# Down's first operands asked for as slots come free, a second buffer for block 21, no block of four pairs, x2 added one product later

## The chip, the cores and the metric

The kernel runs on one core of a Trainium2 chip. The metric is the device time of one execution in microseconds (us); the profile of one execution shows, for each engine, when every instruction ran and what it waited for. PE is the matrix engine, DVE, ACT and POOL are the vector, scalar and GpSimd engines, and SP issues nearly all DMAs, strictly in the order of its queue.

## What is computed

One layer of a decoder trunk on 512 tokens of width 2048, in float32. The part that matters here is the feed-forward network at its end:

```python
x = x + mix @ w_out[l]                      # x2 in the kernel
h2 = _rms_norm(x, norm2_g[l])
x = x + (jax.nn.silu(h2 @ w_gate[l]) * (h2 @ w_up[l])) @ w_down[l]
```

with 5632 hidden columns: `w_gate` and `w_up` are 2048 x 5632, `w_down` is 5632 x 2048. Ahead of it stand a norm, one input projection, three token mixers and the output projection.

## The kernel before

Everything is kept transposed, 128 channels on the partitions and 512 tokens along a row. Each float32 operand is split in a high and a low part; a product is high x (high and low) and low x high. In the feed-forward network the matrix products are done by a seven-product scheme of Strassen's kind: the token axis and the two channel axes are cut in halves, and seven products of halves (numbered q, taken in the order 5 1 7 6 2 4 3) take the place of eight. One product over a "pair" (two 128-channel tiles, one of each half) is one matmul `wh` of 128x512, against the operand's high and low parts side by side, and one `wl` of 128x256.

**Weights.** A block of products needs four weight blocks, named 11, 12, 21 and 22, read from memory into raw buffers of 128x1024, and three sums of them that POOL makes: s = 21 + 22, later s + 11, later s + 12, and 21 + 11 in place (line 184; "s+11" and "s+12" in the text). The seven products take, in order, s, 11, 21, s, 12, 22, s. Each is then split: ACT writes a copy `wn` to PSUM (L248) and `wh` to one of three buffers (L249), and DVE writes `wl` (L229). PE reads wh and wl (L988). A raw buffer is free again once its block has been split for the last time or added. Before the change 22 and s have two buffers (a and b, for even and odd blocks of products), and 21, 11 and 12 have one. `pump` asks SP for the entries in list order (L219), and stops at the first whose buffer is taken.

**Slots.** All other tiles (128x512 float32) come from a pool of 75 slots. A new tile takes a slot that has been given back; its first writer waits until the last user of the old tile is done. An operand load that waits so holds all that is behind it in SP's queue.

**The stages at the end.** Gate/up walks 22 pairs of hidden tiles p in `GU_ORDER`, which ends with 21, 0 and 5; each p is two blocks, g (gate) and u (up), of seven products over the 8 pairs of `ops`, the operand tiles, which stay in 56 slots throughout. The result of a p becomes seven operand tiles a (one per q), which are stored to memory (`od<-a`, L962) one after another as they are computed during the next blocks. Pairs 0 and 5 (`STAY`) are also kept in slots; pair 5 is not stored.

Down then runs 25 blocks d0 to d24, given by the table `DOWN`: (n, first, end) adds the pairs first to end-1 to the output rows n and n+8. Rows 0 to 7 are visited three times (row 0 four times); between visits the partial sums y go to memory and back (`yd<-y` L1121, `y<-yd` L1100). Block d16 is (0, 12, 18), six pairs; d21 is (0, 18, 22), four pairs. At the last visit of a row x2 is loaded (L1103), and POOL adds it to y at the block's start (L1116, L1117), ahead of that block's s+11.

**The order around the change.** The functions run product by product. Ahead of each product come the sums that are due (`sums_now`) and the evacuations of the product before (`evacs`); behind it come `extras`, a second list, with DMAs. `later(n, ...)` puts a call n products further on. In u5, the last gate/up block, each product gives back its eight `ops` slots, and one product later four operands of the same q are loaded for d0 (`load_act`, L1168: pairs 1 to 4 for each q, 28 loads in all). In Down the pairs that the next block adds are loaded likewise, product by product, and y and x2 of the next block are asked for after the fourth product.

Of the kernel before, what the change touches and what calls it, by code (L numbers as in the profile page):

```python
# [9 lines left out]
F32 = mybir.dt.float32  # L10
# [7 lines left out]
T = 512  # L18
# [28 lines left out]

N_SLOTS = 75

RAW_PLAIN = "22b sb 21 22a 11 sa 12".split()  # L50
RAW_BUFS = 7
RAW_EARLY = 5
# [22 lines left out]
        (0, 5, 12), (1, 6, 14), (2, 7, 15), (3, 8, 16), (4, 9, 17), (5, 10, 18), (6, 11, 19), (7, 13, 20),  # L75
        (0, 12, 18), (1, 14, 22), (2, 15, 22), (3, 16, 23), (4, 17, 24), (0, 18, 22), (5, 18, 25), (6, 19, 26), (7, 20, 27)]

# [40 lines left out]
def kernel(ctx: ExitStack, tc: tile.TileContext, xT, wi, wo, wgu, wd, cst_in, outT):  # L118
# [46 lines left out]
    for u, unit in enumerate(units):  # L165
        entries.append((RAW_PLAIN[u % RAW_BUFS], u, [unit]))
        works.append((u, True, nc.vector))

    def group(name, m, n, blocks):

        key = {k: (k, name) for k in ("11", "12", "21", "22", "s")}
        for k in ("21", "22", "11", "12"):
            entries.append((k + "ab"[m] if k == "22" else k, key[k], blocks[k]))
        u = len(works)
# [794 lines left out]
    class Block:  # L969
# [3 lines left out]
        def __init__(self, name, m):  # L973
            self.name = name

            self.banks = dict(zip((5, 1, 7, 6), outs if m == 0 else (outs[3], outs[1], outs[2], outs[0])))
            self.banks.update({3: self.banks[5], 4: self.banks[7], 2: self.banks[1]})

        def multiply(self, q, w, xs):
# [23 lines left out]
    class Wide(Block):  # L1003
# [55 lines left out]
        def piece(self, at, src):  # L1059
# [3 lines left out]
            for k in range(n):  # L1063
                q, s = LAID[at + k], slice(k * TH, (k + 1) * TH)
                t = slot(f"a{q}_{self.p}", F32R)
                nc.scalar.copy(t[:, :TH], src[:, s])
                nc.vector.tensor_sub(t[:, TH:], src[:, s], near[:, s].bitcast(F32))
                if self.p in STAY:
                    acts[q, self.p] = t
                if self.p != STAY[1]:  # L1070
                    later(0, nc.sync.dma_start, od[self.p][:, (at + k) * T:(at + k + 1) * T], t.bitcast(F32),
                          queue=extras)
# [18 lines left out]
    def visit(t):  # L1091

        return [all(w[0] != DOWN[t][0] for w in part) for part in (DOWN[:t], DOWN[t + 1:])]

    def load_y(t):
        if t < len(DOWN):
            for n in (DOWN[t][0], DOWN[t][0] + 8):
                y[t, n] = slot(f"y{t}_{n}")
                if not visit(t)[0]:
                    nc.sync.dma_start(y[t, n], yd[n])  # L1100
                if visit(t)[1]:
                    xr[n] = slot(f"yx{n}")
                    nc.sync.dma_start(xr[n], x2d[n])  # L1103

    class Down(Block):


        def __init__(self, t):
            super().__init__(f"d{t}", t % 2)
            self.n = DOWN[t][0]  # L1110
            self.fresh, last = visit(t)
            self.out = outT if last else yd
            self.tail = t == len(DOWN) - 1
            self.y1, self.y2 = y.pop((t, self.n)), y.pop((t, self.n + 8))
            if last:
                nc.gpsimd.tensor_add(self.y2, self.y2, xr.pop(self.n + 8))  # L1116
                nc.gpsimd.tensor_add(self.y1, self.y1, xr.pop(self.n))  # L1117

        def store(self, n, t, cols):
            def go():  # L1120
                nc.sync.dma_start(self.out[n][:, cols], t[:, cols])  # L1121
            if self.tail:
                go()
            else:
                later(0, go, queue=extras)

# [35 lines left out]
    def load_act(q, pairs):  # L1162
        for j in pairs:
            if (q, j) in acts or j == STAY[1]:
                continue
# [5 lines left out]
    for g in range(2 * NP + len(DOWN)):  # L1171
# [8 lines left out]
        for i, q in enumerate(ORDER):  # L1180
# [10 lines left out]
            if t == -1:  # L1191
                for j in range(NJ):
                    ops.pop((q, j))
                later(1, load_act, q, range(*DOWN[0][1:]), queue=extras)
            elif 0 <= t < len(DOWN) - 1:
                for j in range(FIRST[t], FIRST[t + 1]):
                    acts.pop((q, j))
                later(1, load_act, q, range(LAST[t], LAST[t + 1]), queue=extras)
            if t >= -1 and i == 3:
                load_y(t + 1)  # L1200
# [86 lines left out]
```

## Time and profile before

| | |
|---|---|
| median of 3 runs | 1910.57 us (1910.22 to 1911.08) |
| the profiled execution | 1910.5 us, of it span 1908.7 us |
| PE busy | 1892.0 us, 99% |
| DVE, ACT, POOL busy | 1466.9 us, 1330.1 us, 995.6 us |
| mean granted PE clock | 0.997 |
| DMA | 320.29 MB, mean 168 GB/s |

Gate/up runs up to about 1465 us and Down from there to the end. A row of the timeline gives start, duration, engine, line, operation, output and inputs, shape and count, and in brackets the idle time before it with what ended it. "SPq" is the issue of a DMA, whose duration is not that of the transfer. In the windows a row gives the stretch, PE's busy time, the granted clock (1.00 is full rate), the DMA engines' busy share and GB/s.

### The profile page before, as it was taken

The page shows a single profiled execution, that of the slowest core. Times are in us where ns is not written, and L with a number is a line of the kernel's source. Part 1 is how long each engine was busy: PE and PEld are TensorE (multiplying, and loading weights), DVE is VectorE, ACT ScalarE, POOL GpSimd, SP SyncE. Part 2 cuts the span into 40 slices and gives each one's busy share as a digit, 9 for nine tenths or more (in the row PEclk, how much of TensorE's full clock was granted, in tenths as well). Part 3 has the DMA queues.
Part 4 walks back from the last instruction along what each step waited for, and adds up shares of the span by engine and source line. Part 5 has one row for each costly group of instructions (what it writes and reads, how often), then busy time and mean ns, then how long its engine had stood idle before and what let it go on. Part 6 is the DMA issues. An engine that isn't in the chain of part 4 may idle for free. (4 is left out here: it accounts for less than half of the span.)

```text
span 1908.7 us, 29643 instructions
## 1 busy us (share of the span) xinstructions
PE 1892.0 (99%) x10342; PEld 1639.4 (86%) x10342; DVE 1466.9 (77%) x2561; ACT 1330.1 (70%) x1855; POOL 995.6 (52%) x643
## 2 busy tenths in 40 slices
PE   9999999999999999999999999999999999999999
PEld 7888888878888888888888888888888888888887
DVE  6789988998679777777777777777777777677766
ACT  6356655553357888888888887888887777766765
POOL 0111011000002887787878877788666655655766
PEclk9999999999999999999999999999999999999999
DMA  7342242333332344444435443444438777776876
GB/s 266 88 128 78 83 130 77 110 107 129 117 137 101 124 162 141 160 160 157 158 130 182 147 167 137 161 164 159 152 136 289 248 244 251 272 251 236 294 263 214
DMA packets 136309, 320.29 MB, mean 168 GB/s; under 512 B 15584, under 2 KB 31072, under 8 KB 136160
## 3 DMA queue, kind: packets, MB, share of 16 engines
q1 hardware_dynamic: 136016, 318.31, 49.2%
q8 instruction: 81, 1.33, 0.3%
q14 instruction: 68, 0.56, 0.1%
q10 hardware_dynamic: 144, 0.10, 0.0%
HBM read 254.11 MB, written 55.84 MB: 162 GB/s over the span
## 5 line engine op out<-in xcount | busy, mean ns | idle before, releaser
L988 PE MATMUL out<-h,wh 128*128 128x512 f32 x2464 | 588.8, 391 | 1.0 <-DVE h L899 0.8
L988 PEld LDWEIGHTS out<-h,wh 128*128 128x128 f32 x2464 | 452.7, 188 | 89.3 <-DVE h L899 1.3
L988 PEld LDWEIGHTS out<-h,wl 128*128 128x128 f32 x2464 | 316.0, 191 | 12.0
L988 PE MATMUL out<-h,wl 128*128 128x256 f32 x2464 | 319.9, 283 | 0.0
L988 PE MATMUL out<-a,wh 128*128 128x512 f32 x1232 | 298.4, 392 | 3.8 <-ACT wh L249 2.5
L988 PEld LDWEIGHTS out<-a,wh 128*128 128x128 f32 x1232 | 226.1, 189 | 49.2 <-ACT wh L249 3.3
L242 ACT CAST wh<-w 128x1024 fp32r<-128x1024 f32 (+1 forms) x93 | 96.8, 1041 | 113.9 <-PE o L272 49.0
L988 PEld LDWEIGHTS out<-a,wl 128*128 128x128 f32 x1232 | 161.8, 194 | 8.9 <-DVE wl L229 2.0
L988 PE MATMUL out<-a,wl 128*128 128x256 f32 x1232 | 164.6, 285 | 1.3 <-DVE wl L229 1.2
L229 DVE TENSOR_TENSOR wl<-w,wh 128x1024 fp32r<-128x1024 f32 (+1 forms) x93 | 112.4, 1209 | 44.6 <-ACT wh L242 44.4
L458 DVE SCALAR_TENSOR_TENSOR y<-bu,cst,y 128x511 f32<-128x511 f32 (+14 forms) x120 | 89.6, 747 | 0.2
L1000 DVE TENSOR_TENSOR y<-y,out 128x256 f32<-128x256 f32 x93 | 39.1, 420 | 39.3 <-PE out L988 37.1
L271 PE MATMUL cq<-hh,wh 128*128 128x512 f32 x128 | 51.2, 400 | 0.5 <-DVE mix_c L743 0.5
L271 PE MATMUL o<-mh_c,wh 128*128 128x512 f32 x128 | 51.6, 403 | 0.0
L273 PE MATMUL o<-mh_c,wl 128*128 128x512 f32 x128 | 50.5, 394 | 0.0
L272 PE MATMUL o<-ml_c,wh 128*128 128x512 f32 x128 | 50.4, 394 | 0.0
L273 PE MATMUL cq<-hh,wl 128*128 128x512 f32 x128 | 50.0, 391 | 0.0
L272 PE MATMUL cq<-hl,wh 128*128 128x512 f32 x128 | 50.0, 390 | 0.0
L1001 DVE TENSOR_TENSOR y<-y,out 128x256 f32<-128x256 f32 x101 | 42.5, 421 | 3.5
L386 POOL TENSOR_TENSOR lvr<-lvv,nhalf 128x4 f32<-128x4 f32 x1 | 1.9, 1928 | 76.6 <-DVE lvv L385 76.6
L184 POOL TENSOR_TENSOR w('s', 'g1')_5687<-w('21', 'g1')_5484,w('22', 'g1')_5533 128x1024 f32<-128x1024 f32 x1 | 2.5, 2453 | 71.0 <-DVE wl L229 71.0
L849 DVE TENSOR_TENSOR xr<-xr,o 128x512 f32<-128x512 f32 x32 | 21.8, 682 | 13.8 <-PE o L273 13.7
(3135 smaller groups left out, 4867.4 us busy)
## 6 DMA issues: line engine op xcount, KB each, us to landing
a<-od SPq DMA_DIRECT2D x175, 256.0 KB, 5.4
od<-a SPq DMA_DIRECT2D x147, 256.0 KB, 3.2
w<-in_wi SPq DMA_DIRECT2D x59, 512.0 KB, 3.6
w<-in_wo SPq DMA_DIRECT2D x32, 512.0 KB, 3.5
yd<-y SPq DMA_DIRECT2D x68, 128.0 KB, 3.0
y<-yd SPq DMA_DIRECT2D x34, 256.0 KB, 5.3
x<-in_xT SPq DMA_DIRECT2D x16, 256.0 KB, 7.2
xr<-in_xT SPq DMA_DIRECT2D x16, 256.0 KB, 3.8
```

The source lines that it names most:

```text
L184: eng.tensor_add(out[:, :n], raws[key[a]][0][:, :n], raws[key[b]][0][:, :n])
L229: fn(*args)
L242: nc.scalar.copy(hi[:, :n], t[:, :n])
L271: nc.tensor.matmul(out, wh, xh, start=start, stop=False)
L272: nc.tensor.matmul(out, wh, xl, start=False, stop=False)
L273: nc.tensor.matmul(out, wl, xh, start=False, stop=stop)
L386: nc.gpsimd.tensor_tensor(r, v, nhalf[:, :NT], op=ALU.pow)
L458: nc.vector.scalar_tensor_tensor(yconv[j][:, i:], hconv[j][:, :T - i], c, yconv[j][:, i:], op0=ALU.mult, op1=ALU.add)
L849: nc.vector.tensor_add(t, t, b)
L988: nc.tensor.matmul(out, lhs[:, s], rhs, start=begin, stop=x is xs[-1] and low == flip[0], skip_group_check=True)
L1000: sign(out, out if first is None else first, main)
L1001: sign(out, out, rest)
```

## The change

- The raw buffer of 21 becomes two (21a and 21b), paid for with two slots (73 instead of 75); block 22 stands ahead of 21 in the list.
- The operands of d0 are asked for earlier: those of product 5 during g5, the block before u5; the others during u5's first four products, in the numbers in which the products give back slots.
- Pair 0 is no longer stored in gate/up but product by product during d0, from the slots in which it stays.
- d16 becomes (0, 12, 17) and d21 (0, 17, 22): five pairs each.
- For rows 0 and 8 x2 is added in d8 instead of the last visit; in all blocks that add x2 the additions come one product later, and y and x2 of the next block are asked for after the second product instead of the fourth.
- The stores of y are put one product later.
- The four PSUM banks are handed on from block to block by a rule instead of by the block's parity; the rotation is the same.

```diff
-N_SLOTS = 75
+N_SLOTS = 73
-RAW_PLAIN = "22b sb 21 22a 11 sa 12".split()
-RAW_BUFS = 7
+RAW_PLAIN = "22b sb 21a 22a 11 sa 12".split()
+RAW_BUFS = 8
...
-        (0, 12, 18), (1, 14, 22), (2, 15, 22), (3, 16, 23), (4, 17, 24), (0, 18, 22), (5, 18, 25), (6, 19, 26), (7, 20, 27)]
+        (0, 12, 17), (1, 14, 22), (2, 15, 22), (3, 16, 23), (4, 17, 24), (0, 17, 22), (5, 18, 25), (6, 19, 26), (7, 20, 27)]
...
-        for k in ("21", "22", "11", "12"):
-            entries.append((k + "ab"[m] if k == "22" else k, key[k], blocks[k]))
+        for k in ("22", "21", "11", "12"):
+            entries.append((k + "ab"[m] if k[0] == "2" else k, key[k], blocks[k]))
...
-                if self.p != STAY[1]:
+                if self.p not in STAY:
                     later(0, nc.sync.dma_start, od[self.p][:, (at + k) * T:(at + k + 1) * T], t.bitcast(F32),
...
+        return begin, last, t == 8 if DOWN[t][0] == 0 else last
...
-            if last:
-                nc.gpsimd.tensor_add(self.y2, self.y2, xr.pop(self.n + 8))
-                nc.gpsimd.tensor_add(self.y1, self.y1, xr.pop(self.n))
+            if residual:
+                later(1, self.add_x2)
...
-                later(0, go, queue=extras)
+                later(1, go, queue=extras)
...
-                later(1, load_act, q, range(*DOWN[0][1:]), queue=extras)
+                for k in ((1, 2), (3,), (4, 5), (6,), (), (), ())[i]:
+                    later(0, load_act, ORDER[k], range(*DOWN[0][1:]), queue=extras)
+            elif t == -2 and i == 2:
+                load_act(ORDER[0], range(*DOWN[0][1:]))
             elif 0 <= t < len(DOWN) - 1:
+                if t == 0:
+                    where = slice(LAID.index(q) * T, (LAID.index(q) + 1) * T)
+                    nc.sync.dma_start(od[STAY[0]][:, where], acts[q, STAY[0]].bitcast(F32))
...
-            if t >= -1 and i == 3:
+            if t >= -1 and i == (3 if t < 0 else 1):
                 load_y(t + 1)
```

On PE, DVE and ACT the instructions keep their order; only those of d16 and d21 change in size or number. SP and POOL are reordered. The rows below name tiles as the program does: `a5_1` is the operand of product 5, pair 1; `w('22', 'd0')` is block 22 for d0; `od0` is pair 0 in memory.

SP, at the end of gate/up, before:

```order
L962 DMA od0_5941<-a6_0_14832 128x512
L962 DMA od0_5941<-a4_0_14835 128x512
L219 DMA w('21', 'd0')_14876<-in_wd 128x640
L219 DMA w('22', 'd0')_14878<-in_wd 128x640
L219 DMA w('11', 'd0')_14880<-in_wd 128x640
L1168 DMA a5_1_14927<-od1_5942 128x512
L1168 DMA a5_2_14929<-od2_5943 128x512
```

and now:

```order
L219 DMA w('12', 'u5')_14719<-in_wgu 128x1024
L1175 DMA a5_1_14737<-od1_5946 128x512
L1175 DMA a5_2_14739<-od2_5947 128x512
L1175 DMA a5_3_14741<-od3_5948 128x512
L1175 DMA a5_4_14743<-od4_5949 128x512
L219 DMA w('22', 'd0')_14758<-in_wd 128x640
L219 DMA w('21', 'd0')_14760<-in_wd 128x640
L219 DMA w('11', 'd0')_14882<-in_wd 128x640
L1175 DMA a1_1_14901<-od1_5946 128x512
```

The first operand loads take the place of the six stores of pair 0, right behind u5's last weight block.

SP, at the last operands of d0, before:

```order
L1168 DMA a4_4_15106<-od4_5945 128x512
L219 DMA w('21', 'd1')_15118<-in_wd 128x768
L219 DMA w('22', 'd1')_15120<-in_wd 128x768
L219 DMA w('11', 'd1')_15122<-in_wd 128x768
L1168 DMA a3_1_15134<-od1_5942 128x512
```

and now:

```order
L1175 DMA a4_4_14994<-od4_5949 128x512
L219 DMA w('22', 'd1')_15009<-in_wd 128x768
L219 DMA w('21', 'd1')_15011<-in_wd 128x768
L1175 DMA a3_1_15031<-od1_5946 128x512
L1175 DMA a3_2_15033<-od2_5947 128x512
L1175 DMA a3_3_15035<-od3_5948 128x512
L1175 DMA a3_4_15037<-od4_5949 128x512
L219 DMA w('11', 'd1')_15123<-in_wd 128x768
L1208 DMA od0_5945<-a5_0_14780 128x512
```

Block 11 of d1 now stands behind the operands of product 3, and the first store of pair 0 behind it.

POOL, at d22, before (y22_13 and y22_5 are its partial sums, yx13 and yx5 the x2 rows):

```order
L1144 TENSOR_TENSOR y21_0_19106<-y21_0_19106,d21u_19233 128x256
L1116 TENSOR_TENSOR y22_13_19278<-y22_13_19278,yx13_19280 128x512
L1117 TENSOR_TENSOR y22_5_19274<-y22_5_19274,yx5_19276 128x512
L184 TENSOR_TENSOR w('s', 'd22')_19254<-w('s', 'd22')_19254,w('11', 'd22')_19204 128x896
L184 TENSOR_TENSOR w('s', 'd22')_19254<-w('s', 'd22')_19254,w('12', 'd22')_19241 128x896
```

and now:

```order
L1151 TENSOR_TENSOR y21_0_19046<-y21_0_19046,d21u_19231 128x256
L184 TENSOR_TENSOR w('s', 'd22')_19254<-w('s', 'd22')_19254,w('11', 'd22')_19189 128x896
L1123 TENSOR_TENSOR y22_13_19223<-y22_13_19223,yx13_19225 128x512
L1124 TENSOR_TENSOR y22_5_19219<-y22_5_19219,yx5_19221 128x512
L184 TENSOR_TENSOR w('s', 'd22')_19254<-w('s', 'd22')_19254,w('12', 'd22')_19239 128x896
```

The two x2 additions went from ahead of s+11 to between s+11 and s+12.

More of the change, by code (lines that the diff above doesn't have):

```diff
@@ L165 @@
     for u, unit in enumerate(units):
-        entries.append((RAW_PLAIN[u % RAW_BUFS], u, [unit]))
+        entries.append((RAW_PLAIN[u % len(RAW_PLAIN)], u, [unit]))
         works.append((u, True, nc.vector))
@@ L974, in __init__ @@
             self.name = name
-            self.banks = dict(zip((5, 1, 7, 6), outs if m == 0 else (outs[3], outs[1], outs[2], outs[0])))
+            self.banks = dict(zip((5, 1, 7, 6), outs))
             self.banks.update({3: self.banks[5], 4: self.banks[7], 2: self.banks[1]})
+            outs[:] = [self.banks[q] for q in (6, 2, 4, 3)]
         def multiply(self, q, w, xs):
@@ L1091, in visit @@
     def visit(t):
-        return [all(w[0] != DOWN[t][0] for w in part) for part in (DOWN[:t], DOWN[t + 1:])]
+        begin, last = [all(w[0] != DOWN[t][0] for w in part) for part in (DOWN[:t], DOWN[t + 1:])]
+        return begin, last, t == 8 if DOWN[t][0] == 0 else last
     def load_y(t):
@@ L1100, in load_y @@
                     nc.sync.dma_start(y[t, n], yd[n])
-                if visit(t)[1]:
+                if visit(t)[2]:
                     xr[n] = slot(f"yx{n}")
@@ L1110, in __init__ @@
             self.n = DOWN[t][0]
-            self.fresh, last = visit(t)
+            self.fresh, last, residual = visit(t)
             self.out = outT if last else yd
@@ L1114, in __init__, with add_x2 @@
             self.y1, self.y2 = y.pop((t, self.n)), y.pop((t, self.n + 8))
-            if last:
-                nc.gpsimd.tensor_add(self.y2, self.y2, xr.pop(self.n + 8))
-                nc.gpsimd.tensor_add(self.y1, self.y1, xr.pop(self.n))
+            if residual:
+                later(1, self.add_x2)
+        def add_x2(self):
+            nc.gpsimd.tensor_add(self.y2, self.y2, xr.pop(self.n + 8))
+            nc.gpsimd.tensor_add(self.y1, self.y1, xr.pop(self.n))
         def store(self, n, t, cols):
@@ L1163, in load_act @@
         for j in pairs:
-            if (q, j) in acts or j == STAY[1]:
+            if j in STAY:
                 continue
```

## The prediction

> **What bounds the kernel now.** I read the engine shares on the page first, then the windows of PE, then PE's own waits.
>
> ```profile
> span 1908.7 us, 29643 instructions
> PE 1892.0 (99%) x10342; PEld 1639.4 (86%) x10342; DVE 1466.9 (77%) x2561; ACT 1330.1 (70%) x1855; POOL 995.6 (52%) x643
> 1200.00:1400.00 200.00, 200.00 (x1152) 1.00 0.45 157
> PE a2o L730 <- DVE a2pl L716: 2.5, 1, 2.5
> PE out L988 <- ACT wh L249: 2.5, 2, 2.1
> PE out L988 <- DMA a<-od: 1.3, 4, 0.8
> ```
>
> PE, the matmul engine, is the bound: 16.7 us of the span idle, none of it in a long stretch of gate/up. The L988 waits on DMA a and ACT wh lie in Down. So the prize is what Down loses. Idle time understates it, since a lone matmul counts as busy for its whole latency. I take start-to-start times, calibrated on an undisturbed stretch:
>
> ```profile
> 1505.08 3.36 PE L988 MATMUL out<-a,wh 128*128 128x512 f32 x14
> 1508.28 1.83 PE L988 MATMUL out<-a,wl 128*128 128x256 f32 x14
> 1509.95 2.23 PE L988 MATMUL out<-a,wh 128*128 128x512 f32 x9
> ```
>
> 14 wh matmuls take 3.20 us (0.229 each), 14 wl 1.67 us (0.119 each): 0.348 us per pair and product. Now PE at the three places where Down waits, in order of time:
>
> ```profile
> 1465.50 1.29 PE L988 MATMUL out<-a,wh 128*128 128x512 f32 x5
> ...
> 1474.80 1.55 PE L988 MATMUL out<-a,wh 128*128 128x512 f32 x6
> 1477.15 0.50 PE L988 MATMUL out<-a,wh 128*128 128x512 f32 x1 [0.80 <-DMA a<-od]
> ...
> 1479.48 2.54 PE L988 MATMUL out<-a,wl 128*128 128x256 f32 x11
> 1481.82 2.04 PE L988 MATMUL out<-a,wh 128*128 128x512 f32 x6
> 1484.27 1.65 PE L988 MATMUL out<-a,wh 128*128 128x512 f32 x6 [0.41 <-ACT wh L249]
> 1485.76 1.60 PE L988 MATMUL out<-a,wl 128*128 128x256 f32 x12
> ...
> 1846.85 1.09 PE L988 MATMUL out<-a,wh 128*128 128x512 f32 x4
> 1850.02 2.13 PE L988 MATMUL out<-a,wh 128*128 128x512 f32 x7 [2.08 <-ACT wh L249]
> 1851.95 3.39 PE L988 MATMUL out<-a,wl 128*128 128x256 f32 x14
> ...
> 1860.31 1.10 PE L988 MATMUL out<-a,wl 128*128 128x256 f32 x7 [0.95 <-DVE wl L229]
> 1861.25 3.36 PE L988 MATMUL out<-a,wh 128*128 128x512 f32 x14
> ...
> 1893.71 0.99 PE L988 MATMUL out<-a,wl 128*128 128x256 f32 x7
> 1894.98 1.10 PE L988 MATMUL out<-a,wl 128*128 128x256 f32 x7 [0.28 <-DVE wl L229]
> 1895.92 3.36 PE L988 MATMUL out<-a,wh 128*128 128x512 f32 x14
> ```
>
> - **First**, end of d0, start of d1: 1474.80 to 1485.76 is 10.96 us for 22 wh (6 and 4 single ones, 6, 6) and 11 wl, which need 6.34. Lost: 4.6 us.
> - **Second**, d21 into d22: 1846.85 to 1861.25 is 14.40 us for 25 wh and 28 wl (7 more wl stand between), which need 9.05. Lost: 5.3 us.
> - **Third**, in d24: 14 wl in 2.21 us instead of 1.67. Lost: 0.5 us.
>
> Together 10.5 us. Part of it is the clock:
>
> ```profile
> 1480.00:1482.00 2.00, 2.00 (x11) 0.50 0.40 131
> 1852.00:1854.00 2.00, 1.96 (x9) 0.50 1.05 382
> 400.00:450.00 50.00, 47.23 (x228) 0.97 0.40 113
> ```
>
> Columns: window, its length, PE busy, granted clock, DMA share, GB/s. The clock falls to half right behind the first two stalls (14 wl in 3.39 us at 1851.95 against 1.83: about 1.55 us each time), and the 50 us around the 2.5 us wait at a2o average 0.97. The four waits that open the first stall, one behind the other, lose 2.4 us (1474.80 to 1479.48, less ten wh); the second stall opens with 2.08. The 0.95 us at 1860 and the 0.28 us in d24 bring no fall.
>
> **The change, part by part.** *First stall.* SP issues in order, so I read what stood ahead of the late loads, and who waited for them:
>
> ```profile
> 1434.64 9.02 SPq L962 DMA_DIRECT2D od<-a  x6
> 1449.69 1.85 SPq L1168 DMA_DIRECT2D a<-od  x4
> 1468.82 0.33 SPq L219 DMA_DIRECT2D w('21', 'd1')_15118<-in_wd  x1
> 1470.84 2.33 SPq L1168 DMA_DIRECT2D a<-od  x4
> 1475.58 1.81 POOL L184 TENSOR_TENSOR w('s', 'd1')_15191<-w('21', 'd1')_15118,w('22', 'd1')_15120 128x768 f32<-128x768 f32 x1 [4.50 <-DMA w('22', 'd1')_15120<-in_wd]
> 1483.38 0.83 ACT L249 CAST wh<-w('11', 'd1')_15122 128x768 fp32r<-128x768 f32 x1
> ```
>
> All 28 operand loads (7.3 MB) begin at 1449.69, behind six pair-0 stores that SP issued as their pieces were computed, and last to about 1479 at 382 GB/s (the rate in the second clock row); those of the last product went out at 1470.84 behind d1's weights. The change asks for four of them behind u5's last weight block, that is at 1434.6 where the stores began. The other 24 follow u5's products, whose slots they take: u5 starts at 1465.5 (PE's first "a" matmul) minus 7 x 2.79 = 1446.0, its first product ends at 1448.8, its fourth at 1457.1. From 1448.8, 24 loads (6.3 MB), one 0.3 MB block and two 0.4 MB blocks need 19 us at 382 GB/s: 1468, some 8 us before PE's seventh product of d0 (1465.5 + 6 x 1.74 = 1475.9). So the DMA wait goes. The new waits are on SP: behind the loads that wait for u5's second product (over at 1451.6) stands block 12 of d0, which is first needed in d0, after 1465.5; nothing else is held.
>
> The 0.41 us behind it is a chain: block 22 of d1 late, POOL's sum late by 4.50, ACT's wh ready at 1484.21. With 21 and 22 loaded a block ahead (two buffers, 22 asked for first) the chain moves up by at most those 4.50 us, to 1479.71. PE without the DMA wait needs that wh at 1465.5 + 12.18 + 2.09 = 1479.8: it fits by 0.1 us. That residue costs between nothing and 0.5 + 1.55 us (if the clock fell too). I take 0.5, since 0.41 us brought no fall of its own.
>
> The stores of pair 0 move into d0: seven x 256 KB, beside about 2.3 MB of weights and y (one block of 0.4 MB, three of 0.46, four stores of 0.13). That is 4.1 MB in 12.2 us, 340 GB/s, under the 382 seen; PE's operands for d0 are then there and d1 needs only pair 5, which never leaves. Price 0; if the queue fell behind, d2's blocks would be late and the first stall would come back one block on (4.6 us, the upper bound).
>
> *Second stall.*
>
> ```profile
> 1827.07 2.14 POOL L184 TENSOR_TENSOR w('s', 'd20')_18886<-w('s', 'd20')_18886,w('12', 'd20')_18867 128x896 f32<-128x896 f32 x1 [2.20 <-ACT wh L249]
> ...
> 1839.80 0.81 SPq L219 DMA_DIRECT2D w('21', 'd22')_19198<-in_wd  x2
> 1841.13 1.30 POOL L184 TENSOR_TENSOR w('s', 'd21')_19080<-w('s', 'd21')_19080,w('12', 'd21')_19064 128x512 f32<-128x512 f32 x1 [1.47 <-ACT wh L249]
> 1846.04 2.12 POOL L184 TENSOR_TENSOR w('s', 'd22')_19254<-w('21', 'd22')_19198,w('22', 'd22')_19201 128x896 f32<-128x896 f32 x1 [3.60 <-DMA w('22', 'd22')_19201<-in_wd]
> 1853.59 1.28 POOL L1116 TENSOR_TENSOR y<-y,yx 128x512 f32<-128x512 f32 x1 [1.19 <-DMA yx<-x2d]
> 1856.08 2.12 POOL L184 TENSOR_TENSOR w('s', 'd22')_19254<-w('s', 'd22')_19254,w('11', 'd22')_19204 128x896 f32<-128x896 f32 x1
> ```
>
> Block 21 of d22 could be asked for only when d21 had given up the one buffer, and POOL waited 3.60 us for it. From that sum's start to PE's restart is 1850.02 - 1846.04 = 4.0 us. With a second buffer the blocks are in SBUF a block early, POOL goes on at 1842.43 and PE could have had d22 at 1846.4, before d21's last matmul at 1847.9. The fifth pair lengthens d21 by 2.4 us (d16 shortens by as much, so PE's total is the same) and d21's two x2 additions (1.3 us each) are gone. I price this at -5.3 together with the next edit: s+11 of d22 at 1856.08 stood behind two x2 additions that waited 1.19 us for their data; put ahead of them it starts 3.7 us earlier, more than the 0.95 us that PE waited. The additions now fill the 2.20 us in which POOL waited ahead of s+12; they take 2.58, so s+12 slips 0.4 against s+11, covered by the 3.7. The same swap covers d24's 0.28 (-0.5).
>
> *The rest at nothing*: x2 for rows 0 and 8 added in d8 (2.6 us of POOL, which at 52% has room there; 2.6 us if it had none); y stores one product later (only slots held longer); the banks, the same rotation as before. *Two slots fewer* change which earlier tile a slot waits for all through the first 600 us, which no row prices: between -4.0 (the a2o wait of 2.5 with its clock fall vanishes) and +4.0 (one more like it). I take 0: PE's order there is the same row for row, and a slot's last user is mostly long done.
>
> Sum: the profiled execution took 1910.5 us (span 1908.7, 1.8 around it; the median of the runs is 1910.57). 1910.5 - 4.6 - 5.3 - 0.5 + 0.5 = **1900.6 us**.
>
> **A rule against it.** The clock is half behind a wait of 2.08 us (row above). The Trainium skill, page "TensorE: Matmul & The Clock Gate", Part 1, says that full rate is lost only after an idle window of about 3.4 us, so no wait here should cost clock. By that rule the two falls have another cause and stay, and the sum would be 1903.7, an estimate from the rows' 1.55 us; by the rows, where the falls come right behind the two stalls, it is 1900.6. This trace disagrees with the 3.4 us.
>
> **Rivals.**
> - *One stall stays or is replaced* (0.18). For it: the 0.1 us of room at d1, where ACT and DVE still carry u5's leftover pieces, and a d22 sum that must follow at once. Against: at d21 there are 1.5 us of room. Time: 1910.5 - 5.8 = 1904.7 if the first stays, 1905.9 (-4.6 - 0.5 + 0.5) if the second does.
> - *The clock falls stay though the waits go* (0.04), if they come from something other than the waits: 1900.6 + 2 x 1.55 = 1903.7. Against it: where both stand.
> - *The change moves the waits and not their sum* (0.07): the loads are earlier but SP stops at the next unfinished buffer, and block 11, still single, takes the place of 21: 1910.5.
> - *Slower* (0.09): SP's line. Operand and y loads now ask for a slot as it comes free, from a pool two smaller; a load that waits for PE holds the weight blocks behind it.
>
> ```profile
> 1811.52 0.82 SPq L219 DMA_DIRECT2D w('12', 'd20')_18867<-in_wd  x2
> ```
>
> Block 12 of d20 is issued at 1811.5. A weight block lands within 7 us even when the queue is full (d1's were issued from 1468.82 on, and POOL had them at 1475.58), so this one is there 8 us before POOL adds it at 1827.07. A slot wait must hold SP for over 8 us, more than three products of 2.44, before PE sees it; then each block that is hit costs about what the second stall did, and from two blocks on the gain is gone: three give 1900.6 + 3 x 5.3 = 1916.5. The rows speak against it: the loads ask for slots of products already past.
>
> **Chances.** Forecast 0.62, then as given: 0.18, 0.04, 0.07, 0.09. A measurement of this kernel tells about 0.2% (3.8 us) from no change. Forecast, one stall left and clock falls kept are all faster than 1906.7: 0.84 faster, 0.07 the same, 0.09 slower. The range runs from 1899.0 (no residue at d1, and 1 us of the first part's unknown) to 1906.5 (one stall left): it leaves out the last two rivals and a little of the first part.
>
> **What would show it.** Right: PE's waits on "a<-od" gone; no L988 wait over 0.5 us after 1446; no window at clock 0.50 after 500 us; the first group of four operand loads issued near 1435; POOL's sum of d22 not waiting for a DMA; PE busy still 1892 less the latency counted in stalls. Wrong: a wait on ACT wh or DVE wl at d1 or d22 that is as long as before, a new wait in d2 to d8 or d16, or a longer one at a2o.

## The result and the profile after

The changed kernel takes **1899.49 us** (median of 6 runs, 1899.20 to 1899.99) against 1910.60 us for the kernel before (1909.91 to 1912.15): a ratio of 0.9941, interval 0.9931 to 0.9951. The forecast was 1900.6 us in a range of 1899.0 to 1906.5. The profiled execution took 1899.99 us, 10.5 us less than that of before, which is the whole loss that the prediction had counted in Down.

First the page of the changed kernel (span; busy time, share and instructions of each engine), then PE's own waits (total us, times, longest):

```profile
span 1898.2 us, 29669 instructions
PE 1887.0 (99%) x10342; PEld 1636.9 (86%) x10342; DVE 1467.6 (77%) x2561; ACT 1330.7 (70%) x1855; POOL 996.1 (52%) x643
```

```profile
PE a2o L730 <- DVE a2pl L716: 2.5, 1, 2.5
...
PE out L989 <- DVE h L899: 0.8, 1, 0.8
...
```

Of PE's waits in Down none is left: the DMA line for "a<-od", the 2.1 us for wh and the line for DVE's wl are gone. (A wait of 0.2 us for wh that the profile still lists lies between 600 and 700 us.) The waits at a2o and at h, both ahead of Down, stand as they did. The two instants at which the clock had been 0.50, as windows (from:to, length, PE busy, granted clock, DMA share, GB/s):

```profile
1480.00:1482.00 2.00, 2.00 (x13) 1.00 1.07 353
1852.00:1854.00 2.00, 2.00 (x10) 1.00 1.04 391
```

A start-to-start measure of all of Down will be used for every run below: from PE's first matmul that reads an "a" operand to the start of its last wl group. Here are both ends in the changed kernel, with the place of the old first stall between them (PE's timeline: start, duration, line, operation, count):

```profile
1465.28 1.29 PE L989 MATMUL out<-a,wh 128*128 128x512 f32 x5
...
1478.19 3.14 PE L989 MATMUL out<-a,wh 128*128 128x512 f32 x12
1481.17 1.60 PE L989 MATMUL out<-a,wl 128*128 128x256 f32 x12
...
1893.51 0.99 PE L989 MATMUL out<-a,wl 128*128 128x256 f32 x7
```

Down took 1893.51 - 1465.28 = **428.23 us**; before, 1903.99 - 1465.50 = 438.49. So 10.26 us of the 10.5 came from Down and 0.22 from ahead of it. At d1 twelve wh take 2.98 us start to start instead of 12 x 0.229 = 2.75: the residue is 0.23 us. Down is read from the one profiled execution of each kernel. The kernel before, with its stalls, spreads by several us from execution to execution (1907.2 to 1913.5 in one set of 13), the changed one by less than 1 us above, so a difference in Down is no finer than that spread.

Why the first stall is gone is read from SP's queue (start and duration of the issues, count at the end) and from POOL:

```profile
1434.39 2.08 SPq L1175 DMA_DIRECT2D a<-od  x4
...
1447.44 6.39 SPq L1175 DMA_DIRECT2D a<-od  x12
1454.17 0.33 SPq L219 DMA_DIRECT2D w('12', 'd0')_14962<-in_wd  x1
1454.96 5.51 SPq L1175 DMA_DIRECT2D a<-od  x8
...
1463.29 2.35 SPq L1175 DMA_DIRECT2D a<-od  x4
1466.01 0.33 SPq L219 DMA_DIRECT2D w('11', 'd1')_15123<-in_wd  x1
```

```profile
1470.81 1.86 POOL L184 TENSOR_TENSOR w('s', 'd1')_15189<-w('21', 'd1')_15011,w('22', 'd1')_15009 128x768 f32<-128x768 f32 x1
...
1835.32 2.12 POOL L184 TENSOR_TENSOR w('s', 'd22')_19254<-w('21', 'd22')_19091,w('22', 'd22')_19088 128x896 f32<-128x896 f32 x1
...
1842.39 2.14 POOL L184 TENSOR_TENSOR w('s', 'd22')_19254<-w('s', 'd22')_19254,w('11', 'd22')_19189 128x896 f32<-128x896 f32 x1 [0.39 <-DVE wl L229]
1844.49 1.29 POOL L1123 TENSOR_TENSOR y<-y,yx 128x512 f32<-128x512 f32 x1
```

The last four operand loads leave 7.5 us earlier than before (1470.84), ahead of d1's block 11. POOL's sum for d1 starts at 1470.81 without a wait (before: 1475.58 behind 4.50 us); that for d22 at 1835.32 (before: 1846.04 behind 3.60 us). The x2 additions (L1123) stand behind s + 11 and wait for nothing.

### The profile page after: what moved, and what is told of

It is laid out like the page before. It is cut to its first block, busy times and chain, and to the rows that moved or that the text cites. A ratio compares the mean times of both kernels' runs of the same rounds, so it can differ in the third digit from the quotient of the medians.

```text
span 1898.2 us, 29669 instructions
## 1 busy us (share of the span) xinstructions
PE 1887.0 (99%) x10342; PEld 1636.9 (86%) x10342; DVE 1467.6 (77%) x2561; ACT 1330.7 (70%) x1855; POOL 996.1 (52%) x643
## 4 chain that ended last, share of the span: by engine, by line
PE 94%; DVE 4%; ACT 1%; issue 0%; DMA 0%; SPq 0%; DVEq 0%; ACTq 0%
PE out L989 68%; PE o L271 2%; PE o L272 2%; PE o L273 2%; PE cq L271 2%; PE cq L273 2%; PE cq L272 2%; PE ak L271 1%; PE ak L273 1%; PE ak L272 1%; PE in L272 1%; PE av L271 1%; PE av L272 1%; PE in L273 1%; PE av L273 1%; PE in L271 1%
## 5 line engine op out<-in xcount | busy, mean ns | idle before, releaser
L989 PE MATMUL out<-h,wh 128*128 128x512 f32 x2464 | 588.8, 391 | 1.0 <-DVE h L899 0.8
L989 PEld LDWEIGHTS out<-h,wh 128*128 128x128 f32 x2464 | 452.7, 188 | 89.3 <-DVE h L899 1.3
L989 PEld LDWEIGHTS out<-h,wl 128*128 128x128 f32 x2464 | 316.0, 191 | 12.0
L989 PE MATMUL out<-h,wl 128*128 128x256 f32 x2464 | 319.9, 283 | 0.0
L989 PE MATMUL out<-a,wh 128*128 128x512 f32 x1232 | 296.2, 391 | 0.0
L989 PEld LDWEIGHTS out<-a,wh 128*128 128x128 f32 x1232 | 225.7, 188 | 43.6 <-ACT wh L249 0.4
L989 PEld LDWEIGHTS out<-a,wl 128*128 128x128 f32 x1232 | 159.4, 191 | 6.9
L989 PE MATMUL out<-a,wl 128*128 128x256 f32 x1232 | 161.5, 283 | 0.0
```

Of the source, the lines that this page charges most:

```text
L989: nc.tensor.matmul(out, lhs[:, s], rhs, start=begin, stop=x is xs[-1] and low == flip[0], skip_group_check=True)
```

## Experiments

All runs were compared with the kernel before on the same chip. There the kernel before took 1910.4 to 1911.1 us. "Before" and "changed" name the two kernels. The time is the median of four executions, of ten for the runs with one buffer and with two slots fewer, and of one for the false delay. The same line of code has another number in some of the kernels (PE's L988, L989 and L993 are one line). In the expectations for the old loads, for the old loads and stores and for one buffer of 21, A is the prediction's theory (both edits, each for its part), B that the early loads alone end the first stall, C that the second buffer alone does.

### Is it the order of the loads, or the second buffer of 21?

**Old loads** (changed kernel, operand loads requested as before):

```
- for k in ((1, 2), (3,), (4, 5), (6,), (), (), ())[i]:
-     later(0, load_act, ORDER[k], ...)
- elif t == -2 and i == 2: load_act(ORDER[0], ...)
+ later(1, load_act, q, ...)
```

> The changed kernel (1899.5 us) with d0's 28 operand loads asked for as before, one product after u5's product of the same q; pair 0 is still stored in d0, 21 still has two buffers. Theory A (the prediction's: the loads must be asked for earlier): without the six stores ahead of them the loads begin at about 1448.8 instead of 1449.7, 28 of them and 1.6 MB of weights need 23 us, so the last land near 1472, 4 us before PE's seventh product: at most the 0.2 us at d1 grows to 0.5; 1899.5 to 1900. Theory B (the place of the requests alone took the first stall away): the stall is back, +4.6 us, 1904.1. Theory C (the second buffer of 21 alone did it): 1899.5.

Measured: 1901.85 us, ratio 0.9949 (0.9932 to 0.9967), Down 430.63 us, 2.40 more than in the changed kernel. SP and PE:

```profile
1447.54 2.03 SPq L1175 DMA_DIRECT2D a<-od  x4
1453.79 0.33 SPq L219 DMA_DIRECT2D w('12', 'd0')_14938<-in_wd  x1
1454.16 1.85 SPq L1175 DMA_DIRECT2D a<-od  x4
...
1458.08 11.09 SPq L1175 DMA_DIRECT2D a<-od  x16
1469.53 0.33 SPq L219 DMA_DIRECT2D w('11', 'd1')_15115<-in_wd  x1
```

```profile
1476.50 0.50 PE L989 MATMUL out<-a,wh 128*128 128x512 f32 x1 [0.34 <-DMA a<-od]
...
1482.11 1.66 PE L989 MATMUL out<-a,wh 128*128 128x512 f32 x6 [0.41 <-ACT wh L249]
```

Between 1449.57 and 1453.79 SP issued nothing: it stood at block 12 of d0, whose buffer came free when u5's block 12 had been split and added. DVE's wl of it, to which the profile puts 4.1 us of SP's wait, ended at 1453.65, POOL's last sum of u5 at 1453.75. With the old requests 4 operand loads are out by then, with the new ones 16: in the changed kernel twelve went out between 1447.44 and 1453.83, so slots were free for them. This is read from the two traces; no run moves block 12 alone. No theory had it: A expected at most 0.5 us, B the whole 4.6, C none.

**Old loads, old stores** (the same, with pair 0's seven stores back in the gate and up phase):

```
-                 if self.p not in STAY:
+                 if self.p != STAY[1]:
...
-                 if t == 0: nc.sync.dma_start(od[STAY[0]][:, where], ...)
```

> As e1_old_loads, and pair 0 is stored during gate/up as before, so that six stores stand ahead of the loads again; only 21's second buffer is left of what bears on the first stall. Theory A (requests and stores together set when the loads start, and the weights of d1 ahead of the last loads do the rest): part of the stall is back, since the loads start at 1449.7 but 21 and 22 of d1 no longer hold SP at 1468.8: between 0.5 and 2.5 us, 1900 to 1902. Theory B (start of the loads is all): +4.6 us, 1904.1. Theory C (the second buffer of 21 alone): 1899.5.

Measured: 1903.36 us, ratio 0.9958 (0.9943 to 0.9973), Down 432.28. That is over A's 1900 to 1902, under B's 1904.1 and far from C's 1899.5. Of the 4.6 us of the first stall 4.05 are back, but split otherwise: PE waits five times for a<-od and then 1.01 us for ACT's wh, and the clock does not fall. ACT's wh is late here although 21 and 22 come early. POOL's queue shows why:

```profile
1477.37 1.83 POOL L184 TENSOR_TENSOR w('21', 'd1')_14986<-w('21', 'd1')_14986,w('11', 'd1')_15122 128x768 f32<-128x768 f32 x1 [4.25 <-DMA w('11', 'd1')_15122<-in_wd]
...
1480.65 0.73 POOL L1058 TENSOR_TENSOR u5tb<-u5tb,u5l 128x256 f32<-128x256 f32 x1
```

Block 11 of d1 has taken the place of 21: it stands behind the 16 loads on SP, POOL waits 4.25 us for it, and u5's last piece (u5tb), which ACT converts ahead of wh, waits behind that. This was a rival of the prediction ("block 11, still single, takes the place of 21"). The early requests defeat it, as they bring block 11 forward to 1466.01.

**New loads, old stores** (changed kernel, only the seven stores put back):

> The changed kernel with pair 0's seven stores put back into the gate and up phase; Down's operands are still asked for early, and block 21 keeps two buffers. Theory P (what counts at the first stall is how many operand loads stand on SP ahead of block 12 of d0, 16 with the early requests and 4 with the old ones): the stores are short and go out long before, so 1899.5 to 1900.0, Down within 0.4 us of the changed kernel's 428.23 us. Rival S (the six or seven stores hold the loads up by their transfers, as the prediction's first stall had it; the run with old loads lost another 1.65 us of Down when they were put back): 1900.8 to 1901.5, Down 429.5 to 430.2, with a DMA wait on a<-od again.

Measured: 1899.95 us, ratio 0.9946 (0.9931 to 0.9960), Down 428.25. Theory P holds: with the loads early the place of the stores is worth nothing. With late loads Down was 1.65 us longer with the old stores (432.28 against 430.63), but the executions of those two runs overlap (1901.4 to 1904.5 and 1900.2 to 1903.1), so that this cost is likely and not shown.

**One buffer for 21** (changed kernel, otherwise whole; 21 ahead of 22 again):

```
- RAW_PLAIN = "22b sb 21a 22a 11 sa 12".split()
- RAW_BUFS = 8
+ RAW_PLAIN = "22b sb 21 22a 11 sa 12".split()
+ RAW_BUFS = 7
```

> The changed kernel with one buffer for 21, asked for ahead of 22, as before; all else as changed (73 slots, early loads, five pairs, x2 later). Theory A: at d1 the sum of 21 and 22 starts some 1.5 us later than with two buffers and PE waits about 1.7 us for wh of d1's second product; at d22 21 can be asked for only when d21's third product is split, and PE waits 0 to 1 us; with a clock fall of 1.55 us behind the first: 1901.5 to 1904. Theory C (the second buffer is what counts): both stalls are back, +9.9 us, 1909. Theory B (it does not count once the loads are early): 1899.5.

Measured: 1906.4 us, ratio 0.9977 (0.9968 to 0.9986), Down 435.02, 6.79 more: over A's 1901.5 to 1904 and under C's 1909, while B (1899.5) fails. PE and POOL:

```profile
1478.50 1.55 PE L989 MATMUL out<-a,wh 128*128 128x512 f32 x6
1482.72 2.66 PE L989 MATMUL out<-a,wh 128*128 128x512 f32 x6 [2.67 <-ACT wh L249]
1485.18 2.17 PE L989 MATMUL out<-a,wl 128*128 128x256 f32 x12
...
1852.26 1.10 PE L989 MATMUL out<-a,wl 128*128 128x256 f32 x7 [0.99 <-DVE wl L229]
```

```profile
1473.95 1.85 POOL L184 TENSOR_TENSOR w('s', 'd1')_15189<-w('21', 'd1')_15119,w('22', 'd1')_15121 128x768 f32<-128x768 f32 x1 [3.14 <-DMA w('22', 'd1')_15121<-in_wd]
...
1844.57 2.13 POOL L184 TENSOR_TENSOR w('s', 'd22')_19254<-w('21', 'd22')_19183,w('22', 'd22')_19186 128x896 f32<-128x896 f32 x1 [4.07 <-DMA w('22', 'd22')_19186<-in_wd]
```

At d1 PE's waits for the operands of product 3 are gone and the chain through block 22 stays: 1478.50 to 1485.18 is 6.68 us for twelve wh that need 2.75, and the next twelve wl take 2.00 instead of 1.43: 4.5 us lost, as much as all of the first stall before. So either edit without the other leaves half of the stall or more (2.40 or 4.05 us with two buffers, by the place of the stores, 4.5 with early loads); only both together end it. At d22, though, POOL's wait of 4.07 us, longer than the 3.60 of before, costs PE one wait of 0.99 us and no clock: PE's groups lag those of the changed kernel by 4.58 us behind d1's stall (1487.18 against 1482.60), by 5.14 in d21 (1836.71 against 1831.57) and by 6.75 behind this wait (1853.20 against 1846.45), so d22 lost 1.6 us. (The 0.56 between came at d17, with a wait of 0.3 us for a<-od.)

**The old table** (changed kernel with d16 of six pairs and d21 of four):

```
- (0, 12, 17) ... (0, 17, 22)
+ (0, 12, 18) ... (0, 18, 22)
```

> The changed kernel with d16 of six and d21 of four pairs as before. Theory A (the four-pair block is too short in itself: DVE has seven splits and the evacuations, 4 x 0.68 + 3 x 1.09 + 5.7 = 11.7 us of work in a block of 9.8): PE waits 1 to 2 us at d22, perhaps with a clock fall: 1900.5 to 1903. Theory C (with two buffers of 21 POOL's sum for d22 follows at once and the short block is covered): 1899.5. A return of the whole second stall: 1904.8.

Measured: 1899.4 us, ratio 0.9938 (0.9923 to 0.9953), Down 428.23: not a hundredth of a microsecond from the changed kernel. A (1900.5 to 1903) fails and C holds: the fifth pair of d21 is worth nothing once 21 has two buffers, with the rest of the change in place.

### The second buffer by itself

**Before, with the second buffer** (22 ahead of 21, eight blocks, 73 slots; nothing else):

> The kernel before with the second buffer for block 21 alone (22 ahead of 21, eight blocks, 73 slots); old requests, old stores, old table, x2 added at its old place, y stores as before. Theory P (two buffers end the second stall and the ACT half of the first; the late a3 operands stay, 4 us of Down, as in the run with old loads and old stores): no POOL wait for block 22 of d22, Down 432.0 to 432.6, 1903.2 to 1903.8. Rival X (the DVE wait of 0.95 us at d22 came from the x2 adds ahead of s+11 and needs them moved): 1904.2 to 1906, with a wait of PE for DVE's wl at d22. Rival N (two buffers pay only together with the early loads): 1908 or more.

Measured: **1929.97 us**, ratio 1.0100 (1.0085 to 1.0115). The second buffer, done alone, makes the kernel 19.4 us slower. Down takes 457.88 us. P and X (1903 to 1906) fail; N's "1908 or more" holds the number, but its cause, the missing early loads, is not what the run with y and x2 moved shows below. PE's waits in its last blocks are new:

```profile
1817.44 2.90 PE L988 MATMUL out<-a,wh 128*128 128x512 f32 x7 [2.78 <-ACT wh L249]
...
1856.87 2.07 PE L988 MATMUL out<-a,wh 128*128 128x512 f32 x4 [5.18 <-ACT wh L249]
...
1876.93 1.86 PE L988 MATMUL out<-a,wl 128*128 128x256 f32 x7 [4.42 <-DVE wl L229]
```

POOL waited 28.2 us in six waits for x2 (before: 11.8 in eight). POOL and SP over one block of this run:

```profile
1777.35 2.42 POOL L184 TENSOR_TENSOR w('s', 'd17')_18282<-w('s', 'd17')_18282,w('12', 'd17')_18264 128x1024 f32<-128x1024 f32 x1 [2.45 <-DVE wl L229]
...
1790.62 1.28 POOL L1116 TENSOR_TENSOR y<-y,yx 128x512 f32<-128x512 f32 x1 [4.45 <-DMA yx<-x2d]
...
1793.10 2.11 POOL L184 TENSOR_TENSOR w('s', 'd18')_18484<-w('s', 'd18')_18484,w('11', 'd18')_18412 128x896 f32<-128x896 f32 x1
1797.42 2.14 POOL L184 TENSOR_TENSOR w('s', 'd18')_18484<-w('s', 'd18')_18484,w('12', 'd18')_18466 128x896 f32<-128x896 f32 x1 [2.21 <-DVE wl L229]
```

```profile
1779.79 0.33 SPq L219 DMA_DIRECT2D w('12', 'd18')_18466<-in_wd  x1
1781.99 0.81 SPq L219 DMA_DIRECT2D w('22', 'd19')_18496<-in_wd  x2
...
1785.26 0.38 SPq L1103 DMA_DIRECT2D yx<-x2d  x1
...
1799.59 0.81 SPq L219 DMA_DIRECT2D w('12', 'd19')_18665<-in_wd  x2
...
1819.94 0.81 SPq L219 DMA_DIRECT2D w('12', 'd20')_18867<-in_wd  x2
```

This is a closed ring over two in-order queues. POOL's s + 12 of d17 ends at 1779.77 and frees the buffer of 12, so SP issues 12 of d18 at 1779.79. Next in SP's line stand the blocks 22 and 21 of d19, which the second buffer now lets it take; 22 waits until d17's 22 is done with, 1781.99. Only then come the loads of y and x2, the last one 5.5 us behind block 12. POOL, which has the x2 additions ahead of s + 11, stands until 1790.62. Its s + 12 comes behind s + 11 and the split of that sum (the 2.21 us for DVE's wl), so it ends at 1799.56, and SP issues 12 of d19 at 1799.59. One turn takes 19.8 us, the next 20.35. PE needs 7 products x 7 pairs x 0.348 = 17.05 us for such a block, so the ring is slower than PE, and PE falls behind it block by block. Before, the x2 loads of that block went out 0.9 and 1.9 us behind block 12 (1778.08, then 1778.98 and 1779.93), and its last turns took 17.8 and 17.7 us.

**Two slots fewer** (before, with 73 slots in place of 75), to part the slots from the ring:

> The kernel before with 73 slots in place of 75 and nothing else. Theory X: nothing, 1910 to 1911.5, x2 waits of POOL as before (11.8 us in 8). Rival S (the slots): 1914 to 1930, with x2 loads late and PE waits after 1770 us.

Measured: 1911.66 us, ratio 1.0005 (0.9996 to 1.0014): nothing that can be measured. The slots are not the cause. The profiled execution of it has a Down of 440.78 us, 2.29 more than that of the kernel before. The waits at d22 came out otherwise there: the first, 1.66 us in place of 2.08, left the clock at 1.00, and the wait for DVE's wl that is 0.95 us in the kernel before is 2.30 us and brought it down:

```profile
1861.17 1.86 PE L988 MATMUL out<-a,wl 128*128 128x256 f32 x7 [2.30 <-DVE wl L229]
```

So what the second stall costs differs by some 2 us between two executions of nearly the same program.

**Second buffer with y and x2 moved** (the run of 1930 us, with y and x2 asked for at the second product and the additions queued one product later):

```
-             if t >= -1 and i == 3:
+             if t >= -1 and i == (3 if t < 0 else 1):
...
-                 nc.gpsimd.tensor_add(self.y2, ...) (at the start of the block)
+                 later(1, self.add_x2)
```

> The kernel before with the second buffer for block 21 (as in the run that took 1930 us), and in Down y and x2 asked for at the second product of a block in place of the fourth and the x2 adds queued one product later; old operand requests, old stores, old table, bank order and y stores of before. Theory X (the second buffer lets SP take the next block's 22 and 21 ahead of the x2 loads, SP stands there until the 22 buffer is free, and POOL, whose x2 adds stand ahead of s + 11, stands in its turn; x2 earlier and its adds later take both away): no POOL wait for x2 above 1 us, the waits of PE after 1770 us gone, what is left is the first stall: Down 432.0 to 432.8, 1903.2 to 1904.2. Rival S (two slots fewer are what held Down up): still 1915 or more. Rival M (only a part is mended, since d21 adds x2 of block column 0 as before): 1905 to 1912.

Measured: 1903.01 us, ratio 0.9958 (0.9943 to 0.9973), Down 431.21; POOL has no wait for x2 and PE no wait after d1. These two edits alone take 27 us off the run of 1930. What is left to the changed kernel's 428.23 is 2.98 us at d1, the first stall as in the runs with old loads.

**Which of the two edits breaks the ring?** The changed kernel with the additions back at the start of a block, and, apart from it, with y and x2 asked for at the fourth product again:

> The changed kernel with the x2 adds queued at the start of a block, ahead of s + 11, as before; y and x2 are still asked for at the second product. Theory X: POOL now starts the adds some 3.5 us earlier, about when x2 lands (1768.12 us + 5.6 us for the first), so POOL waits 1 to 2 us in some blocks and s + 11 comes 4 us later: PE waits for wl of 0.5 to 1.5 us in one to four blocks, 1900.3 to 1904, with no fall of the clock unless one passes 1.7 us. Rival E (with the loads early the place of the adds is nothing): 1899.5. Rival L (the place of the adds is what carries it): 1908 or more.

> The changed kernel with y and x2 asked for at the fourth product of a block as before, behind the next block's 22 and 21 on SP; the x2 adds stay one product later. Theory X: x2 of d18 is asked for at about 1774 in place of 1768.12 us, lands at 1780 and is wanted at 1778.56; POOL waits 1 to 5 us for x2 in most of the last blocks, but has 1 to 4 us idle in each, so PE loses 0 to 3 us: 1899.5 to 1902.5. Rival E (early loads are what carries it): 1908 or more, with PE waits in d18 to d24. Rival A (the adds' place carries it alone): 1899.5.

Measured: 1899.69 us (ratio 0.9938, 0.9922 to 0.9955; Down 428.23) and 1899.56 us (0.9939, 0.9924 to 0.9954; Down 428.22). Either edit alone is enough in the changed kernel. The changed kernel without both was not run; what that costs is known only from the kernel before with the second buffer. In the first run POOL never waits for x2. In the second it does (POOL's timeline):

```profile
1779.54 1.29 POOL L1123 TENSOR_TENSOR y<-y,yx 128x512 f32<-128x512 f32 x1 [2.51 <-DMA yx<-x2d]
...
1798.54 1.30 POOL L1123 TENSOR_TENSOR y<-y,yx 128x512 f32<-128x512 f32 x1 [3.80 <-DMA yx<-x2d]
```

18.6 us in seven waits, more than in the kernel before, and PE loses none of it: the additions stand behind s + 11 there, and what waits behind them is s + 12 alone. So the total of POOL's waits says nothing here; what stands behind each wait does.

### What brings the clock down

**A false delay on DVE** (changed kernel; ahead of the wl of the fourth product of d9 to d15, 9 to 17 repeats of the first 256 columns of the same subtraction):

```
+ for _ in range(dose.get(u - len(units), 0)):
+     nc.vector.tensor_sub(lo[:, :TH], t[:, :TH], near[:, :TH].bitcast(F32))
```

> The changed kernel with a false delay on DVE: ahead of the wl of the fourth product of d9 to d15 the first 256 columns of that same subtraction are done 9, 10, 11, 12, 13, 15 and 17 times more (about 0.42 us each, 3.8 to 7.1 us), so that PE waits for wl for a growing time, once a block. The output stays as it is. Theory A (the granted clock falls to 0.50 after any single wait above some 2 us): waits under 1.2 us cost themselves alone, each of 2 to 3 us costs some 1.55 us on top, seen as wh and wl groups of 16 at twice their time. Rival R (only a wait above 3.4 us does it): no fall below 3.4 us; the falls at 2.08 to 2.67 us came from something else that they had in common.

Measured: 1909.2 us in a single execution, Down 438.71. Four of the seven delays reached PE:

```profile
1641.28 1.21 PE L993 MATMUL out<-a,wl 128*128 128x256 f32 x8 [0.37 <-DVE wl L229]
...
1681.78 1.21 PE L993 MATMUL out<-a,wl 128*128 128x256 f32 x8 [1.29 <-DVE wl L229]
1682.83 3.81 PE L993 MATMUL out<-a,wh 128*128 128x512 f32 x16
1686.48 2.08 PE L993 MATMUL out<-a,wl 128*128 128x256 f32 x16
...
1723.71 2.08 PE L993 MATMUL out<-a,wl 128*128 128x256 f32 x8 [2.65 <-DVE wl L229]
1725.59 4.57 PE L993 MATMUL out<-a,wh 128*128 128x512 f32 x16
...
1747.46 3.46 PE L993 MATMUL out<-a,wl 128*128 128x256 f32 x14 [1.87 <-DVE wl L229]
```

Behind 0.37 and 1.29 us PE runs on at full rate. Behind 2.65 us the next eight wl and sixteen wh take 6.28 us start to start where they took 4.70 behind 1.29: 1.58 us more. Behind 1.87 us the fourteen wl take 3.46 instead of 1.83. R does not hold: the clock fell behind waits well under 3.4 us. In Down all single waits of all runs sort by length: no fall behind 0.37, 0.98, 0.99, 1.01, 1.16, 1.29, 1.64 and 1.66 us, a fall behind 1.87, 2.08, 2.30, 2.65, 2.67, 2.78, 4.42 and 5.18. But A's "any single wait above some 2 us" does not hold either. All profiled executions but one have the same wait of 2.53 to 2.56 us at a2o, ahead of Down; in eleven the clock fell behind it, in two it did not, and this run is one of the two. The other is the run with y and x2 late, whose wait ends at the same instant (416.72) as in the changed kernel. Behind it, in the changed kernel first and then in that run:

```profile
418.00:421.00 3.00, 3.00 (x12) 0.53 0.00 0
418.00:421.00 3.00, 3.00 (x17) 1.00 0.03 5
```

Without the fall Down starts at 1463.71 in place of 1465.28, 1.57 us earlier, which is what the fall costs. Why two of thirteen were spared no run shows.

### The attention product one tick later

PE's longest wait that is left, 2.5 us at a2o with a clock fall behind it, has nothing to do with the change. One run moved that product a tick later:

```
- A_TICKS = (0, 8, 2, 1, 3, 1, 3, 1, 2)
+ A_TICKS = (0, 8, 2, 1, 3, 1, 3, 1, 3)
```

> Not a test of the change: the changed kernel with the product of attention weights and values of the a rows put one tick later (last number of A_TICKS 3 in place of 2), where PE still waits 2.5 us for a2pl and the clock falls after it. If the wait ends there and nothing else comes late: 2.5 + 1.5 = 4 us less, 1895.5. If a3's row, the last one, then ends later: 1899 to 1901.

Measured: **1897.38 us**, ratio to the kernel before 0.9932 (0.9915 to 0.9948), on another occasion than the 1899.49 of the changed kernel, and with an interval that overlaps that one's (0.9931 to 0.9951). In the same set the run with old stores, which has the Down of the changed kernel, took 1898.9 to 1900.7, all above this run's 1897.0 to 1897.7; so it is likely some 2 us faster, half of the 4 us hoped for. The wait at a2o and the 0.5 us at a3o are gone, and a new wait stands elsewhere:

```profile
PE o L271 <- DVE mix_a L743: 1.9, 1, 1.9
```

The output projection now waits for the mix of a row. The 50 us around it (400 to 450 us) still average a clock of 0.97, so a fall stays too, behind 1.88 us.

| Run | us | Down, us |
|---|---|---|
| before | 1910.6 | 438.49 |
| before, 73 slots | 1911.66 | 440.78 |
| before, second buffer of 21 | 1929.97 | 457.88 |
| the same, y and x2 moved | 1903.01 | 431.21 |
| changed, one buffer of 21 | 1906.4 | 435.02 |
| changed, old loads and stores | 1903.36 | 432.28 |
| changed, old loads | 1901.85 | 430.63 |
| changed, old stores | 1899.95 | 428.25 |
| changed, old table | 1899.4 | 428.23 |
| changed, additions at the start | 1899.69 | 428.23 |
| changed, y and x2 late | 1899.56 | 428.22 |
| changed | 1899.49 | 428.23 |
| changed, false delay | 1909.2 | 438.71 |
| changed, weights product later | 1897.38 | 428.24 |

## Why the prediction was right

The sum was right to 1.1 us, and its method held: start-to-start times on the bound engine gave the prize (10.5 us), and 10.26 us of it came out of Down. Its steps one by one:

- **The first stall, -4.6 us: right, in both halves.** The loads go out by 1465.64 and no wait on a<-od is left. It needed both edits, as the prediction had it; the runs that undo one, alone or with a neighbour, keep 2.4 to 4.5 us. What made the old loads late was only partly what the prediction read, six stores ahead of them. With the stores moved away and the old requests 2.40 us are still lost, by the traces because SP stands at block 12 of d0 with 4 loads ahead of it. The prediction named that block, but asked only whether the block itself comes in time. Its sum for the old loads does not come out either: 7.3 MB at 382 GB/s from 1449.69 on would be over at 1469, not at 1479. The windows from 1449.7 to 1479 of the kernel before add up to 10.4 MB, weight blocks of d0 and d1 among them.
- **The residue at d1, +0.5 us: mis-sized, 0.23 measured.** ACT's wh, priced to be ready at 1479.71 at the earliest, was ready at 1479.62.
- **The stores of pair 0 at nothing: right** (428.25 against 428.23).
- **The second stall, -5.3 us: right in size, too narrow in cause.** The prediction gave the late 21 the clock fall and the 2.08 us, and the place of the additions only the 0.95 us behind them. With a single buffer and the rest of the change, POOL waits longer for 22 of d22 than before, 4.07 us, and PE loses 1.6 us. With the second buffer and nothing else the last blocks get worse by far. So the x2 loads and additions, the part with the small price, carry more than the text gave them. How much of the way from 5.3 to 1.6 belongs to these and how much to the fifth pair of d21 was not tried, and no run has them alone with the kernel before; with two buffers the fifth pair is worth nothing. The 5.3 itself is the reading of one execution, and the run with 73 slots lost some 2 us more there.
- **The third, d24, -0.5 us: right in size, its cause not shown.** The wait of 0.28 us is gone, but it is gone as well where the additions stand at the start of the block, so their swap alone is not what covers it.
- **y and x2 asked for earlier: the step that was missing.** The text prices the order of additions against s + 11 and nothing for when x2 is asked for. That edit and the later additions, which have the small price, are each a full guard in the changed kernel against a ring that costs 27 us in the kernel before with the second buffer. That the sum came out right owes to a guard being in the change for another reason, and was luck in so far.
- **Two slots fewer at 0, bounds -4.0 and +4.0: right** in the kernel before, 1.0005 (0.9996 to 1.0014).
- **Clock falls: right.** They went with the waits, and the 1903.7 us of the rule is not what was measured. The Trainium skill, page "TensorE: Matmul & The Clock Gate", Part 1, has full rate lost after an idle window of about 3.4 us; here it is lost behind single waits from 1.87 us on, kept up to 1.66, and kept twice behind 2.53 and 2.56 us. That a wait of 2.08 us costs clock, as the prediction took it, is what mostly happens here and not a rule.
- **The slower rival, SP's line held: its mechanism is real**, and it is what the second buffer does by itself. Its place and size were off. The prediction looked for cover at block 12 (8 us) and found it ample; the load without cover was x2. It gave 1916.5 us, the run took 1930.
- **Block 11 in the place of 21: real too.** In two runs with two buffers and old loads the profile names it (POOL waits 4.25 us with the old stores, 4.65 us in the run of 1930). In the other two POOL waits 2.57 and 3.16 us at the same sum, but the profile names DVE there.

## What to carry to other kernels

A second buffer does not only bring its own load forward: on an in-order queue it moves that load, with whatever it has to wait for, ahead of all that stood behind, so price the load that is next in the line and the engine that adds it. Look for rings over two in-order queues (here POOL frees 12, SP takes 12, then 22, then x2, POOL adds x2, then frees 12) and compare one turn with the bound engine's time for a block: turns of 17.8 and 17.7 us brought PE no wait in those blocks beside its 17.05, turns of 20 us went with 19.4 us lost in all. And test an edit that is priced at nothing by taking it away, alone and with its neighbour: each of the two guards looked worthless while the other stood.

## What the runs showed of the hardware that was not expected

- Single waits of PE up to 1.66 us cost only themselves. Behind waits of 1.87 to 2.78 us the granted clock fell to half, for some 1.6 us more, in all cases but two, and these two had 2.53 and 2.56 us, the very wait that brought a fall in eleven other executions. So a length between 1.66 and 1.87 us is where falls begin here, and not where they become certain. Behind longer waits more is lost: behind 4.42 us, seven wl and fourteen wh took 6.87 us start to start (1876.93 to 1883.80) instead of the 4.14 behind 1.64 us in the same run (1797.33 to 1801.47).
- Several short waits can do it too: the four that open the first stall of before lost 2.4 us within 4.7 us and the clock fell, four at the same place in the run with old loads lost 1.9 us within 4.2 us (1474.61 to 1478.84, less ten wh) and it did not.
